# Feed-forward of a hybrid mixer block in two passes over all tokens, with the second mixer sweep between the first pass's column tiles

## The chip, the cores and the metric

The kernel runs on one core of a Trainium2 chip. The metric is the device time of one launch in microseconds (us), the median over the runs of the kernel. Below, TensorE (PE in the profile) does matrix products, VectorE (DVE) and GpSimd (POOL) elementwise work, ScalarE (ACT) activations and copies, and SyncE (SP) issues most DMA transfers.

## What is computed

One layer over x of 2048 tokens by 1024 features: three token mixers on slices of one input projection (a convolution module, a state-space scan "SSD" in both directions, pooling), one output projection, then a gated feed-forward with a 3x3 depthwise convolution on the grid of 32 rows by 64 tokens. Each half ends in a layer norm. Shortened:

```
def _conv_ffn(h, lp, rows, width):
    b, L, _ = h.shape
    val, gate = jnp.split(h @ lp['w_up'], 2, axis=-1)
    gate = _dwconv2d(gate.reshape(b, rows, width, D_FF), lp['ffn_dw_w'], lp['ffn_dw_b']).reshape(b, L, D_FF)
    return (val * jax.nn.gelu(gate)) @ lp['w_down']
...
        mix_x, _, _ = _mixer(_modulate(x, shx1, scx1), lp, st_f, st_b)
        x = _layer_norm(DEEPNORM_ALPHA * x + gx1 * mix_x, ln1_g[l], ln1_b[l])
        f_x = _conv_ffn(_modulate(x, shx2, scx2), lp, rows, GRID_W)
        x = _layer_norm(DEEPNORM_ALPHA * x + gx2 * f_x, ln2_g[l], ln2_b[l])
```

Here `D_FF` is 2816, so `w_up` is 1024 x 5632 and `w_down` is 2816 x 1024. `_mixer` concatenates the three mixers' outputs (256 + 512 + 256 features) and multiplies them by `w_out` (1024 x 1024).

## The kernel before

Tokens are worked on in four chunks of 512 (numbers 0 to 3), in sub-chunks of 128 for the scan. Features lie in tiles of 128 partitions. Every large product is done in three matmuls (`mm3`): each float32 operand is split into a high part (a copy by ScalarE in the matmul's input format) and a low part (the rest, by GpSimd or VectorE), and high by high, high by low and low by high are summed in PSUM. Weights come through `load_w`: SP loads 512 KB into a raw tile (`wr`, two buffers), ScalarE writes `wh`, GpSimd `wl` (three buffers each).

The first sweep goes up through the chunks: input projections, convolutions, the forward scan, pooling. It leaves the forward scan's result (`yf`), the convolution's and pooling's outputs (`yac`) and the scan's inputs (`ub`) in DRAM scratch. The second sweep goes down, chunk 3 to 0. `bwd` runs the backward scan: `first(s)` prepares sub-chunk s, `rest(s)` finishes it, norms, and transposes it (`yt`) into `ybh`/`ybl`. `yac` loads and splits the other mixers' features (`yah`, `yal`). `mix` does the output projection into tiles `o` (two halves of 512 columns by four token tiles), adds the residual (`mix`, `xt`), norms, and transposes (`ht`) into the scratch `h2T`, the feed-forward's input.

Then `ffn_chunk` runs once for each chunk, 3 to 0, all its work in one go. `ffn_h2` reloads `h2T` and splits it (`h2h`, `h2l`, 576 tokens: the chunk and one grid row). For each of 22 column tiles: the gate product `ug` (24 matmuls), its copy into `gbuf`, which holds ten grid rows, nine convolution taps in a PSUM tile `fa` (the first by ScalarE, L863, eight by VectorE, L867), gelu into `fg`, the value product `uv` (24 matmuls) and `g = uv * fg` (L875). Gate rows that the next chunk needs are kept in `gcar`. All 22 tiles of g stay in SBUF. Then the down projection: two halves of 512 columns, in each four PSUM tiles `d` and 22 blocks k, for which ScalarE writes `gh` and VectorE `gl` (L897; three buffers each), 12 matmuls a block. At the end VectorE multiplies by the gate row (`fm`, L911), adds to the residual `r` (L912), and norms (L781, L918, L919). The residual tiles are loaded from scratch and scaled (L882 to L884).

The kernel is written on a framework that gives every tile its semaphores and orders each engine's instructions itself, from a timeline of its own; each engine, SP's list of DMAs among them, then runs its list strictly in that order. So the position of a step on each engine is set at build time, not in the source.

Of the kernel before, what the change touches and what calls it, by code (L numbers as in the profile page):

```python
# [7 lines left out]
F32 = mybir.dt.float32  # L8
# [40 lines left out]
class Kern:  # L49
# [3 lines left out]
    def run(self):  # L53
        tc, t = self.tc, self.t
        with ExitStack() as es:
# [3 lines left out]
            self.mm = es.enter_context(tc.tile_pool(name="mm", bufs=4, space=PSUM))  # L59
            for n, b in (("si", 1), ("so", 2), ("lo", 1)):  # L60
                setattr(self, n, es.enter_context(tc.tile_pool(name=n, bufs=b, space=PSUM)))
            self.consts()
            e1, e2, e3 = ExitStack(), ExitStack(), ExitStack()
            self.sp = e1.enter_context(tc.tile_pool(name="sp", bufs=2))
            self.ssd_consts()
            e4, e5 = ExitStack(), ExitStack()
            self.pc = e5.enter_context(tc.tile_pool(name="pc", bufs=2, side="right"))
            self.mod_first()
            self.p1 = e4.enter_context(tc.tile_pool(name="p1", bufs=2))
            self.sweep1()  # L70
            e5.close()
            self.pa = e2.enter_context(tc.tile_pool(name="pa", bufs=2, side="right", reuse_waits="tile"))
            self.ngr = self.row(self.pa, t["norm_row"], "ngr")
            top = self.bwd(NCH - 1)
            e4.close()
            self.p2 = e2.enter_context(tc.tile_pool(name="p2", bufs=2, side="right", reuse_waits="tile"))
            last = self.sweep2(top)
            e1.close()
            self.p3 = e3.enter_context(tc.tile_pool(name="p3", bufs=2, reuse_waits="tile"))
            self.mix(*last)  # L80
            pre = self.ffn_pre()
            e2.close()
            self.p4 = e3.enter_context(tc.tile_pool(name="p4", bufs=2, side="right", reuse_waits="tile"))
            self.ffn(pre)
            e3.close()

# [104 lines left out]
    def mod_half(self, q):  # L191
        nc, t, p1 = self.nc, self.t, self.p1
        acc = self.lp.tile([P, 512], F32, tag="c31", name=f"macc{q}", bufs=4)
        for k in range(KD):
            w = self.lp.tile([P, 512], F32, tag="c31", name=f"wm2_{q}_{k}", bufs=4)
# [13 lines left out]
    def mod_finish(self):  # L209
# [8 lines left out]
        for r, o in ((0, 0), (1, 24)):  # L218
# [19 lines left out]
    def proj(self, w, hs, n, name):  # L238
        ps = self.bank(self.mm, f"ps_{name}")
        for k in range(KD):  # L240
            a = [v[:, k * P : (k + 1) * P] for v in w]
            self.mm3(ps[:, :n], a, [v[:, :n] for v in hs[k]], k == 0, k == KD - 1)
        return ps
# [14 lines left out]
    def dt_path(self, hs, n, key, name):  # L258
# [5 lines left out]
        raw = sp.tile([40, 512], F32, tag="dtraw", name=f"dtr_{name}", bufs=1)  # L264
# [402 lines left out]
    def sweep2(self, top):  # L667
        p2, t = self.p2, self.t
        self.g1r = self.row(p2, self.s["g1"], "g1r")
        for c in reversed(range(NCH)):  # L670
            cur = (c, self.yac(c, top if c == NCH - 1 else self.bwd(c)))
            if c < NCH - 1:
                self.mix(*prev)
# [370 lines left out]
```

## Time and profile before

| | us |
|---|---|
| median of 2 runs | 2694.12 |
| lowest and highest | 2692.11, 2696.13 |
| span of the profiled execution | 2696.6 |
| second sweep, output projection and transposes | 842 to 1158 |
| feed-forward | 1158 to 2676 |
| last norm and stores | 2676 to 2696.6 |

The profiled execution's span is 2.5 us above the median and inside 0.1% of it; times below come from it. The rows of the profile have us from its start. A group row gives line, engine, operation, output and inputs, shapes and count, then busy time, the mean duration of one in ns, and the idle time of the engine ahead of it. The letter q after an engine's name marks its queue, which issues DMAs. TensorE overlaps successive matmuls, so a single one lasts longer than the pitch between two.

### The profile page before, as it was taken

How to read it: one execution, taken by the hardware profiler on the slowest of the kernel's cores; microseconds unless marked ns; L12 is line 12 of the kernel's file. 1: busy time of each engine (PE TensorE's matmuls, PEld its weight loads, DVE VectorE, ACT ScalarE, POOL GpSimd, SP SyncE). 2: the span in 40 equal slices, each digit the busy share in tenths (PEclk: the TensorE clock that was granted, in tenths of full speed). 3: DMA queues.
4: the chain of work that ended last, by engine and by line, in shares of the span. 5: the costliest groups of instructions: out<-in, count | busy, mean ns of one | idle time of the engine just before them, and what ended most of it. 6: DMA issues, size and time to landing. Idle time of an engine off the chain costs nothing.

```text
span 2696.6 us, 31426 instructions
## 1 busy us (share of the span) xinstructions
PE 2452.2 (91%) x11274; PEld 1989.8 (74%) x11274; DVE 1940.6 (72%) x2621; ACT 1132.2 (42%) x1737; POOL 1394.7 (52%) x928
## 2 busy tenths in 40 slices
PE   6886987979877989899999999999999999989996
PEld 3674765757656777688998878878878888878885
DVE  5999997997977965668555496655596664876645
ACT  2544446455645434433334323334333343233342
POOL 3536456565654664645446455455454464555444
PEclk7897998989988999899999999999999999999998
DMA  7653324233345565572234343333343343433332
GB/s 266 198 170 110 101 94 141 88 112 118 99 150 202 164 227 199 158 257 86 87 94 122 94 147 95 94 109 112 94 148 94 94 117 94 156 92 97 101 94 70
DMA packets 125837, 347.00 MB, mean 129 GB/s; under 512 B 19680, under 2 KB 24176, under 8 KB 125680
## 3 DMA queue, kind: packets, MB, share of 16 engines
q1 hardware_dynamic: 121072, 336.60, 39.9%
q10 hardware_dynamic: 4608, 8.39, 1.0%
q8 instruction: 88, 1.44, 0.2%
q14 instruction: 69, 0.57, 0.1%
HBM read 298.63 MB, written 46.31 MB: 128 GB/s over the span
## 4 chain that ended last, share of the span: by engine, by line
PE 55%; DVE 11%; DMA 3%; POOL 2%; issue 1%; ACT 1%; ACTq 0%; SPq 0%; POOLq 0%; DVEq 0%
PE d L108 6%; PE d L110 6%; PE d L109 6%; PE ug L108 5%; PE ug L109 5%; PE ug L110 5%; PE uv L108 5%; PE uv L110 5%; PE uv L109 5%; PE o L108 1%; PE o L109 1%; PE o L110 1%; DVE rq_l L119 1%; DVE fa L867 1%; DVE xt L764 1%
## 5 line engine op out<-in xcount | busy, mean ns | idle before, releaser
L867 DVE SCALAR_TENSOR_TENSOR fa<-gbuf,cols,fa 128x512 f32<-128x512 f32 x704 | 524.2, 753 | 236.1 <-ACT fa L863 200.2
L897 DVE TENSOR_TENSOR gl<-g,gh 128x512 fp32r<-128x512 f32 x176 | 197.2, 1129 | 230.8 <-ACT gh L896 213.5
L96 POOL TENSOR_TENSOR wl_d<-wr_d,wh_d 128x1024 fp32r<-128x1024 f32 x88 | 217.6, 2473 | 229.9 <-ACT wh_d L95 229.8
L96 POOL TENSOR_TENSOR wl_uv<-wr_uv,wh_uv 128x1024 fp32r<-128x1024 f32 x88 | 222.4, 2527 | 202.4 <-ACT wh_uv L95 202.4
L96 POOL TENSOR_TENSOR wl_ug<-wr_ug,wh_ug 128x1024 fp32r<-128x1024 f32 x88 | 217.2, 2468 | 207.4 <-ACT wh_ug L95 207.4
L108 PE MATMUL ug<-h2h,wh_ug 128*128 128x512 f32 (+3 forms) x880 | 311.0, 353 | 14.6 <-DVE g L875 12.5
L109 PE MATMUL ug<-h2l,wh_ug 128*128 128x512 f32 (+3 forms) x880 | 310.0, 352 | 0.0
L110 PE MATMUL ug<-h2h,wl_ug 128*128 128x512 f32 (+3 forms) x880 | 309.7, 352 | 0.0
L108 PE MATMUL uv<-h2h,wh_uv 128*128 128x512 f32 x704 | 278.8, 396 | 8.4 <-DVE g L875 7.8
L108 PE MATMUL d<-wh_d,gh 128*128 128x512 f32 x704 | 278.7, 396 | 1.2 <-ACT fg L869 1.2
L109 PE MATMUL uv<-h2l,wh_uv 128*128 128x512 f32 x704 | 278.7, 396 | 0.0
L110 PE MATMUL uv<-h2h,wl_uv 128*128 128x512 f32 x704 | 278.7, 396 | 0.0
L109 PE MATMUL d<-wl_d,gh 128*128 128x512 f32 x704 | 277.7, 394 | 0.0
L110 PE MATMUL d<-wh_d,gl 128*128 128x512 f32 x704 | 267.7, 395 | 0.0
L573 DVE SCALAR_TENSOR_TENSOR c<-gl,cols,c 128x512 f32<-128x512 f32 (+1 forms) x240 | 252.7, 1071 | 2.1 <-ACT c L571 1.1
L896 ACT ACTIVATE gh<-g 128x512 fp32r<-128x512 f32 x176 | 110.9, 630 | 268.1 <-PE d L109 242.6
L108 PEld LDWEIGHTS ug<-h2h,wh_ug 128*128 128x128 f32 x880 | 167.5, 190 | 37.4 <-DVE g L875 14.2
L95 ACT ACTIVATE wh_ug<-wr_ug 128x1024 fp32r<-128x1024 f32 x88 | 93.2, 1059 | 227.5 <-PE uv L109 206.4
L109 PEld LDWEIGHTS ug<-h2l,wh_ug 128*128 128x128 f32 x880 | 167.5, 190 | 20.4
L110 PEld LDWEIGHTS ug<-h2h,wl_ug 128*128 128x128 f32 x880 | 167.4, 190 | 19.0
L95 ACT ACTIVATE wh_uv<-wr_uv 128x1024 fp32r<-128x1024 f32 x88 | 93.3, 1060 | 164.1 <-PE ug L109 116.8
L108 PEld LDWEIGHTS uv<-h2h,wh_uv 128*128 128x128 f32 x704 | 132.9, 189 | 39.0 <-DVE g L875 8.2
(376 smaller groups left out, 5629.9 us busy)
## 6 DMA issues: line engine op xcount, KB each, us to landing
wr_ug<-in_w_up SPq DMA_DIRECT2D x88, 512.0 KB, 3.6
wr_uv<-in_w_up SPq DMA_DIRECT2D x88, 512.0 KB, 3.6
wr_d<-in_w_dn SPq DMA_DIRECT2D x88, 512.0 KB, 3.6
wm<-in_w_mod SPq DMA_DIRECT2D x64, 256.0 KB, 3.0
wr_x<-in_w_x SPq DMA_DIRECT2D x32, 512.0 KB, 3.7
wr_o<-in_w_o SPq DMA_DIRECT2D x32, 512.0 KB, 4.5
wm<-in_w_mod SPq DMA_DIRECT2D x16, 512.0 KB, 8.4
x_c<-in_xT SPq DMA_DIRECT2D x32, 256.0 KB, 3.7
```

Source lines behind the costliest of these rows:

```text
L95: nc.scalar.activation(hi, src, AF.Copy)
L96: nc.gpsimd.tensor_tensor(lo, src, hi.bitcast(F32), AL.subtract)
L108: nc.tensor.matmul(out, a[0], b[0], start=first, stop=False)
L109: nc.tensor.matmul(out, a[0], b[1], start=False, stop=False)
L110: nc.tensor.matmul(out, a[1], b[0], start=False, stop=last)
L119: nc.vector.tensor_tensor(q, r, r, AL.mult)
L573: nc.vector.scalar_tensor_tensor(acc[:, :n], gl[:, j, k : k + n], w[k], acc[:, :n], AL.mult, AL.add)
L764: nc.vector.scalar_tensor_tensor(xs[i][:, hsl], xs[i][:, hsl], ALPHA, m, AL.mult, AL.add)
L867: nc.vector.scalar_tensor_tensor(acc, G[:, dr : dr + 8, dc : dc + GW], wc[i], acc, AL.mult, AL.add)
L896: nc.scalar.activation(gh, gt[k], AF.Copy)
L897: nc.vector.tensor_tensor(gl, gt[k], gh.bitcast(F32), AL.subtract)
```

## The change

The feed-forward is cut in two passes over all tokens. Pass 1, `ffn_up`, goes through chunks 3, 2, 1, 0: gate, convolution and value product of each column tile, and g is stored to DRAM (`gs`). So that no row of the next chunk is needed, a chunk's convolution and value product are shifted by 128 tokens: chunk 3 does 384 tokens of its own, chunks 2 and 1 do 512, of which 128 belong to the chunk above, and chunk 0 does 640 as two spans of 320. Three gate rows pass from chunk to chunk through DRAM (`gc`, tile `car`). The input tiles `h2h`, `h2l` hold 640 tokens and have 12 buffers. Pass 2, `ffn_down`, again goes through 3 to 0: it reads g from DRAM once for each half of the columns, and has all eight PSUM banks for `d`. The row broadcasts (`g2r`, `agr`, `abr`, `l2g`, `l2b`) are loaded between the passes.

The backward scan and output projection of chunk 3 run alone ahead of pass 1. Those of chunks 2, 1, 0 become a generator, `back`, of which one step is taken after each column tile of the chunk before. In it the output projection is by features: eight tiles `ps_o_f` of 128 features by 512 tokens, with the residual taken from x transposed (`rt`), the gate a column (`g1a`), and four transposes each (`rT`) back to token rows. `yac` has one buffer. Scan inputs are loaded per sub-chunk.

```
+            hs = self.ffn_h2(NCH - 1)
+            for c in reversed(range(NCH)):
+                side = self.back(c - 1) if c else iter(())
+                for _ in self.ffn_up(c, hs):
+                    next(side, None)
+                for _ in side:
+                    pass
+                if c:
+                    hs = self.ffn_h2(c - 1)
...
+                self.banks(e6, (("dn", 8),))
+                self.p4 = e6.enter_context(tc.tile_pool(name="p4", bufs=2, reuse_waits="tile"))
+                self.ffn_rows()
+                for c in reversed(range(NCH)):
+                    self.ffn_down(c)
...
     def yac(self, c, cat):
...
-            yr = p2.tile([P, 512], F32, tag="yac", name=f"yac{c}_{j}")
+            yr = self.mx.tile([P, 512], F32, tag="yac", name=f"yac{c}_{j}", bufs=1)
...
+        rt = []
+        for f in range(8):
+            x = self.mx.tile([P, 512], F32, tag="rt", name=f"rt{c}_{f}", bufs=3)
+            nc.sync.dma_start(x, t["xT"][f, :, cs])
+            ps = self.proj(self.load_w(t["w_o"][f], f"o{c}_{f}"), cat, CH, f"o{c}_{f}", (0, 1, 6, 7, 2, 3, 4, 5))
+            nc.vector.scalar_tensor_tensor(x, ps, self.g1a[:, f : f + 1], x, AL.mult, AL.add)
+            rt.append(x)
+            if f:
+                turn(f - 1)
+            yield
...
+    def ffn_up(self, c, hs):
+        nc, t, p3 = self.nc, self.t, self.p3
+        n = CH if c == NCH - 1 else CH + P
+        v0 = P if c else 0
+        spans = [(v0, n - v0)] if c else [(0, n // 2), (n // 2, n // 2)]
         for f in range(NF):
...
+            nc.sync.dma_start(self.s[f"gs{c}"][f, :, v0:CH], g[:, 0 : CH - v0])
+            if n > CH:
+                nc.sync.dma_start(self.s[f"gs{c + 1}"][f, :, 0:P], g[:, CH - v0 : n - v0])
+            yield
...
+                    g = p4.tile([P, 512], F32, tag="gr", name=f"gr{c}_{hf}_{k}", bufs=6)
+                    nc.sync.dma_start(g, self.s[f"gs{c}"][k])
                     gh = p4.tile([P, 512], F32R, tag="gh", name=f"gh{c}_{hf}_{k}", bufs=3)
                     gl = p4.tile([P, 512], F32R, tag="gl", name=f"gl{c}_{hf}_{k}", bufs=3)
-                    nc.scalar.activation(gh, gt[k], AF.Copy)
-                    nc.vector.tensor_tensor(gl, gt[k], gh.bitcast(F32), AL.subtract)
+                    nc.scalar.activation(gh, g, AF.Copy)
+                    nc.vector.tensor_tensor(gl, g, gh.bitcast(F32), AL.subtract)
```

PSUM, eight banks of 512 columns, was shared as mm 4, si 1, so 2, lo 1; in pass 1 it is mm 3, cv 2 (the convolution's), si 1, so 1, lo 1. SP's list grows from 845 to 1315 entries, TensorE's shrinks from 10345 to 10197, and ScalarE's table loads go from 39 to 55.

What the change does to the order shows at three places. In these rows a name with numbers is a tile (`g_8` the g of column tile 8, `wr_ug_10` the raw gate weights of tile 10), and `scr_` marks DRAM scratch. First SP's list where the row broadcasts are loaded. Before, in the first chunk of the feed-forward:

```order
L775 DMA scr_h2T_63<-h_0_4_9185 128x512
L775 DMA scr_h2T_63<-h_0_5_9193 128x512
L664 DMA g2r<-scr_g_59 128x1024
L664 DMA agr<-in_ln_rows 128x1024
L664 DMA abr<-in_ln_rows 128x1024
L664 DMA l2g<-in_ln_rows 128x1024
L664 DMA l2b<-in_ln_rows 128x1024
L775 DMA scr_h2T_63<-h_0_6_9201 128x512
L775 DMA scr_h2T_63<-h_0_7_9209 128x512
L882 DMA r_3_0_11602<-scr_x1n_82 128x1024
```

And in the new kernel, at the end of pass 1:

```order
L882 DMA scr_gs_65<-g_21_17565 128x512
L884 DMA scr_gs_73<-g_21_17565 128x128
L685 DMA g2r<-scr_g_59 128x1024
L685 DMA agr<-in_ln_rows 128x1024
L685 DMA abr<-in_ln_rows 128x1024
L685 DMA l2g<-in_ln_rows 128x1024
L685 DMA l2b<-in_ln_rows 128x1024
L892 DMA r_3_0_17646<-scr_x1n_88 128x1024
L892 DMA r_3_1_17650<-scr_x1n_88 128x1024
L892 DMA r_3_2_17654<-scr_x1n_88 128x1024
L892 DMA r_3_3_17658<-scr_x1n_88 128x1024
L905 DMA gr_0_0_17672<-scr_gs_89 128x512
```

The five broadcasts and four loads of r, which stood among the transposed tiles' stores and the up weights, now stand behind the store of the last g of pass 1 and ahead of the first g that pass 2 reads.

Second, VectorE's list at the end of a chunk's down projection. Before, chunk 3's norm, with the next chunk's first convolution tile behind it (`fa`):

```order
L918 SCALAR_TENSOR_TENSOR r_3_0_11602<-r_3_0_11602,mv_l_3_0_12489,l2g 128x1024
L783 BN_AGGR mv_l_3_2_12525<-st_l_3_2_12522 128x2
L115 TENSOR_SCALAR rv_l_3_1_12510<-mv_l_3_1_12507 128x1
L918 SCALAR_TENSOR_TENSOR r_3_1_11606<-r_3_1_11606,mv_l_3_1_12507,l2g 128x1024
L783 BN_AGGR mv_l_3_3_12543<-st_l_3_3_12540 128x2
L119 TENSOR_TENSOR rq_l_3_0_12496<-rr_l_3_0_12494 128x1
L918 SCALAR_TENSOR_TENSOR r_3_2_11610<-r_3_2_11610,mv_l_3_2_12525,l2g 128x1024
L867 SCALAR_TENSOR_TENSOR fa_0_12648<-gbuf_9270,cols,fa_0_12648 128x512
L918 SCALAR_TENSOR_TENSOR r_3_3_11614<-r_3_3_11614,mv_l_3_3_12543,l2g 128x1024
```

In the new kernel, the same end of chunk 3 in pass 2:

```order
L803 BN_STATS st_l_3_0_18618<-r_3_0_17646 128x6
L909 TENSOR_TENSOR gl_0_2_18761<-gr_0_2_18758,gh_0_2_18760 128x512
L923 TENSOR_TENSOR fm_1_3_18615<-d_1_3_18143,g2r 128x512
L803 BN_STATS st_l_3_1_18636<-r_3_1_17650 128x6
L924 TENSOR_TENSOR r_3_2_17654<-r_3_2_17654,fm_1_2_18612 128x512
L805 BN_AGGR mv_l_3_0_18621<-st_l_3_0_18618 128x2
L909 TENSOR_TENSOR gl_0_3_18779<-gr_0_3_18776,gh_0_3_18778 128x512
L924 TENSOR_TENSOR r_3_3_17658<-r_3_3_17658,fm_1_3_18615 128x512
L805 BN_AGGR mv_l_3_1_18639<-st_l_3_1_18636 128x2
L803 BN_STATS st_l_3_2_18654<-r_3_2_17654 128x6
L134 TENSOR_SCALAR rv_l_3_0_18624<-mv_l_3_0_18621 128x1
L930 SCALAR_TENSOR_TENSOR r_3_0_17646<-r_3_0_17646,mv_l_3_0_18621,l2g 128x1024
```

Between the norm's instructions now stand the `gl` of the next chunk's down projection, in place of the taps `fa`.

Third, SP's list where a side chunk's `yac` tiles are loaded, in the new kernel (the other mixers' features of chunk 1, during pass 1 of chunk 2):

```order
L882 DMA scr_gs_81<-g_8_10647 128x384
L884 DMA scr_gs_89<-g_8_10647 128x128
L854 DMA car_14_11358<-scr_gc_90 128x192
L700 DMA yac_0_10680<-scr_yac_70 128x497
L702 DMA yac_0_10680<-scr_yac_78 128x15
L775 DMA rt_0_10709<-in_xT 128x512
L775 DMA rt_1_10826<-in_xT 128x512
L775 DMA rt_2_10949<-in_xT 128x512
L728 DMA zsr_3_12623<-scr_zs_61 128x512
L700 DMA yac_1_10687<-scr_yac_70 128x497
L702 DMA yac_1_10687<-scr_yac_78 128x15
L700 DMA yac_6_10694<-scr_yac_70 128x497
```

And TensorE's list at the start of that projection:

```order
L129 MATMUL uv_8_128_10648<-h2h_7_9588,wl_uv_8_10643 128x512
L369 MATMUL bps_b_3_12398<-ident,ubr_3_12385 128x128 x2
L372 MATMUL bps_b_3_12398<-ubr_3_12385 128x128 x2
L428 MATMUL yd_b_0_10561<-xdt_b_0_10326,E_b_0_10298 128x64 x8
L127 MATMUL ps_o_0_10717<-yah_0_10683,wh_o_0_10712 128x512
L127 MATMUL ug_9_10751<-h2h_0_9539,wh_ug_9_10746 128x512
```

In before the loads of `yac_0` (here of chunk 0) stood among loads of x and output weights:

```order
L749 DMA xt_2_7606<-in_x 128x1024
L749 DMA xt_3_7608<-in_x 128x1024
L683 DMA yac_0_8356<-scr_yac_62 128x497
L685 DMA yac_0_8356<-scr_yac_68 128x15
L683 DMA yac_1_8363<-scr_yac_62 128x497
L685 DMA yac_1_8363<-scr_yac_68 128x15
L102 DMA wr_o_0_3_8426<-in_w_o 128x1024
```

What moved: the `yac` loads now stand behind the store of the g of tile 8, and TensorE comes to the first matmul of `ps_o_0` between the value product of tile 8 and the gate product of tile 9.

307 lines of the change are left out of this document (140 added, 167 removed).

## The prediction, made before the changed kernel was run

> **What bounds the kernel now.** I read the totals first, then the stretches after the first sweep, then the chain of waits through them, and last the groups of instructions by line. The page's totals:
>
> ```profile
> span 2696.6 us, 31426 instructions
> PE 2452.2 (91%) x11274; PEld 1989.8 (74%) x11274; DVE 1940.6 (72%) x2621; ACT 1132.2 (42%) x1737; POOL 1394.7 (52%) x928
> ```
>
> TensorE is the bound: a change pays where it removes TensorE's idle time, and costs where it makes some. The stretches (the first number after the span is its length, then PE, PEld, DVE, ACT and POOL busy, the granted clock, the DMA share, GB/s):
>
> ```profile
> 842.00:1158.00 316.00, 279.51 (x1356) 227.71 (x1356) 222.15 (x391) 131.86 (x255) 178.97 (x125) 0.93 0.60 199
> 1158.00:1240.00 82.00, 76.26 (x458) 69.09 (x459) 64.05 (x93) 30.42 (x44) 39.06 (x27) 0.98 0.56 184
> 1482.80:1550.20 67.40, 67.40 (x291) 54.21 (x290) 30.80 (x36) 26.56 (x36) 29.35 (x12) 1.00 0.33 95
> 1550.20:1617.60 67.40, 62.91 (x262) 50.41 (x261) 63.34 (x85) 19.39 (x24) 35.15 (x20) 0.95 0.45 148
> 1752.40:1819.80 67.40, 66.24 (x284) 53.00 (x284) 39.65 (x54) 25.87 (x34) 34.71 (x26) 1.00 0.38 108
> 1954.60:2022.00 67.40, 62.94 (x260) 50.57 (x259) 63.53 (x80) 22.76 (x30) 35.59 (x25) 0.95 0.47 148
> 2359.00:2426.40 67.40, 59.79 (x264) 50.95 (x265) 53.29 (x73) 25.42 (x34) 34.84 (x28) 0.95 0.32 91
> ```
>
> The third row is dense: 291 matmuls in 67.40 us, a pitch of 0.2316 us for 512 columns. The first is the second sweep. Its output projection alone, the same view of tile `o`, and its first 38 us:
>
> ```profile
> 842.00:1158.00 316.00, 204.49 (x768) 147.12 (x768) 18.80 (x29) 0.93 0.60 199
> ...
> 842.00:880.00 38.00, 31.70 (x151) 26.19 (x152) 27.30 (x44) 18.56 (x46) 19.49 (x16) 0.87 0.61 214
> ```
>
> Dense, the 768 would take 768 x 0.2316 = 177.9 us; everything else there was busy for 279.5 - 204.5 = 75.0. So the sweep loses at least 316 - 177.9 - 75.0 = 63 us. The start of the feed-forward lost 82.0 - 76.3 = 5.7. The chunk boundaries, by matmuls missing against the dense row, lost 29, 7 and 31 pitches, so 6.7, 1.6 and 7.2 us; the last one idled 67.4 - 59.8 = 7.6. Together 92 us.
>
> **What the change removes.** The side work of chunks 2, 1, 0 (backward scan, output projection, transposes) now stands between matmuls of the first pass, and a chunk's last column tile no longer precedes its down projection. I book all 92 us as removed: 2696.6 - 92 = 2604.6. The waits that return are put back one by one.
>
> **What it adds to TensorE's work.** The output projection by features needs 128 more transposes (8 tiles x 4 x 4 chunks). Pieces of the chain of waits:
>
> ```profile
> 1186.15 0.87 PE ht L772 x8
> ...
> 1202.74 1.28 ACT L869
> 1204.04 0.61 ACT fg L869
> 1204.66 0.70 DVE g L875
> ```
>
> Eight transposes took 0.87 us, so 128 take 14: 2618.6. Shifting by 128 tokens narrows chunk 3's value matmuls to 384 columns and makes chunk 0's 2 x 320. The gate rows by form (mean ns last before the idle column):
>
> ```profile
> L108 PE MATMUL ug<-h2h,wh_ug 128*128 128x512 f32 x352 | 141.4, 402 | 8.9 <-DVE g L875 8.9
> L108 PE MATMUL ug<-h2h,wh_ug 128*128 128x256 f32 x176 | 50.4, 286 | 3.6 <-DVE g L875 3.6
> ```
>
> That is 0.45 ns a column: 22 x 24 x 128 columns less is 31 us, and 31 more in chunk 0. Net 0.
>
> **The waits that it makes, in five places.** Durations are from these groups (count, busy us, mean ns), from two moments of VectorE's timeline, and from issue-to-landing times (the last number, us):
>
> ```profile
> L867 DVE SCALAR_TENSOR_TENSOR fa<-gbuf,cols,fa 128x512 f32<-128x512 f32 x704 | 524.2, 753 | 236.1 <-ACT fa L863 200.2 <-PE ug L110 13.6
> L96 POOL TENSOR_TENSOR wl_ug<-wr_ug,wh_ug 128x1024 fp32r<-128x1024 f32 x88 | 217.2, 2468 | 207.4 <-ACT wh_ug L95 207.4
> L897 DVE TENSOR_TENSOR gl<-g,gh 128x512 fp32r<-128x512 f32 x176 | 197.2, 1129 | 230.8 <-ACT gh L896 213.5 <-PE d L109 15.1 <-PE d L110 1.5
> L119 DVE TENSOR_TENSOR rq_l<-rr_l 128x1 f32<-128x1 f32 x32 | 30.2, 945 | 2.7 <-POOL rr_l L117 2.7
> L884 DVE TENSOR_TENSOR r<-r,abr 128x1024 f32<-128x1024 f32 x16 | 28.7, 1811 | 0.0
> L919 DVE SCALAR_TENSOR_TENSOR r<-r,rs_l,l2b 128x1024 f32<-128x1024 f32 x12 | 27.2, 2290 | 0.0
> L912 DVE TENSOR_TENSOR r<-r,fm 128x512 f32<-128x512 f32 x28 | 22.7, 810 | 0.0
> L911 DVE TENSOR_TENSOR fm<-d,g2r 128x512 f32<-128x512 f32 x32 | 21.5, 682 | 16.9 <-PE d L110 16.9
> L883 DVE TENSOR_TENSOR r<-r,agr 128x1024 f32<-128x1024 f32 x16 | 21.5, 1361 | 0.0
> L781 DVE BATCH_NORM_STATS2 st_l<-r 128x6 f32<-128x512 f32 x32 | 21.1, 670 | 0.0
> L918 DVE SCALAR_TENSOR_TENSOR r<-r,mv_l,l2g 128x1024 f32<-128x1024 f32 x12 | 20.9, 1742 | 0.0
> ```
>
> ```profile
> 1545.58 0.69 DVE L897 TENSOR_TENSOR gl<-g,gh 128x512 fp32r<-128x512 f32 x1 [1.65 <-ACT gh L896]
> ...
> 1563.01 1.27 DVE L918 SCALAR_TENSOR_TENSOR r<-r,mv_l,l2g 128x1024 f32<-128x1024 f32 x1
> ...
> 1569.76 3.28 DVE L918 SCALAR_TENSOR_TENSOR r<-r,mv_l,l2g 128x1024 f32<-128x1024 f32 x1
> ```
>
> ```profile
> wr_ug<-in_w_up SPq DMA_DIRECT2D x88, 512.0 KB, 3.6
> ...
> scr_h2T<-h SPq DMA_DIRECT2D x32, 256.0 KB, 4.0
> h2r<-scr_h2T SPq DMA_DIRECT2D x32, 256.0 KB, 3.1
> ...
> yac<-scr_yac SPq DMA_DIRECT2D x12, 248.5 KB, 3.8
> ```
>
> ```profile
> L95 ACT ACTIVATE yah<-yac x16: 613/630/636, 841.2 to 1057.8; 128x512 fp32r<-128x512 f32 x16
> L96 POOL TENSOR_TENSOR yal<-yac,yah x16: 1257/1292/1796, 841.9 to 1058.5; 128x512 fp32r<-128x512 f32 x16
> ```
>
> *1. Chunk 3 alone.* Its scan and projection still have no cover. The first 38 us of the sweep idled 6.3 and ran at 0.87 of the clock (4.9): 11 us come back. Then LayerNorm stands open:
>
> ```profile
> 928.20 0.69 DVE mix L763
> ...
> 946.89 0.33 PE ht L772
> ```
>
> From the end of a projection to the first transpose took 18.7 us; the residual arithmetic in it (about 6) now mostly runs tile by tile, so 13. Store, load and split of the first tile (4.0 + 3.1 + 1.3) make 8, and 3 us of half clock after the pause: 24. Taken 35; low 25 (the pause covered like other transposes), high 48 (18.7 in full, the store at 9).
>
> *2. Starts of chunks 2, 1, 0.* SP now puts each h2T store and its reload in one order. After the last transpose the way back takes about 10 us (0.7 + 4.0 + 0.7 + 3.1 + 1.3), and some 36 matmuls (8 us) stand there to cover it, but with the earlier tiles also late. Low 5 in all (the start in the trace lost 5.7); high 30 (10 each); taken 12, nearer the measured start.
>
> *3. `yac` before the side projections.* In SP's order the load of yac_0 stands behind the store of g_8, and its tile has one buffer. g_8 comes 8.5 us after ug_8 (copy and first tap as two more ScalarE passes of 0.6, eight taps 6.0, gelu 0.6, product 0.7), or 9.8 with a table load of 1.28 ahead of gelu, where scan functions ran between; TensorE has 7.7 us until the first projection matmul (24 matmuls of uv_8, 5.6, and scan work for about 2), so g_8 is 0.8 to 2.1 late, taken 1.5; three issues 1.0, landing 3.8, split 0.6: 6.9 us idle. The next three loads follow each other at 3.8 + 0.4 + 0.6 + 1.3 = 6.1, so 18.4, against 58 matmuls x 0.2316 = 13.4: 5 more. Taken 12 for each of three chunks, 36. Low 0 (queues ahead of TensorE); high 60 (8 us more, by loads that land late).
>
> *4. From pass 1 to pass 2.* SP issues the store of g_21, then five row broadcasts and four r loads, and only then gr_0_0: nine times 512 KB, 4.72 MB. In before the same nine stood under dense work:
>
> ```profile
> 1190.00:1215.00 25.00, 22.79 (x135) 20.21 (x135) 20.70 (x27) 12.06 (x19) 11.05 (x9) 1.00 0.85 297
> ```
>
> At 297 GB/s they take 15.9 us; g_21 comes 4.5 us after the last matmul (1.2 + 16 taps of 0.56, see below, + 0.6 + 0.7, so 11.5 after ug_21, less 48 value matmuls of 320 columns at 0.145, 7.0), two issues 0.8, gh and gl 1.8, half clock 1: taken 24. Low 15 (rows land beside each other and gr early); high 33 (VectorE does its four L893 and three L894, 10.9 us, ahead of gl_0_0). The Trainium skill, page "DMA: Bandwidth & Descriptors", section "Specifications", gives about 358 GB/s for one core: an estimate of 13.2 us, 2.7 less in the sum. The row is an average over 25 us and doesn't contradict it.
>
> *5. Pass 2's chunk boundaries.* Before, convolutions of the next chunk gave VectorE 5.6 us of matmuls between them; now every block of 12 matmuls (2.78 us) needs a gl. In the new order, up to gl_0_13, VectorE does 4 x (0.682 + 0.810 + 0.670 + 1.742 + 2.290 + 0.945) + 2 x (1.361 + 1.811) = 34.9 us and 12 gl, 13.5: 48.4 against 13 blocks, 36.1. TensorE waits 12 us at each of three boundaries: 36. Low 0 (below); high 54 (all four r of the next chunk ahead, 6 more each). The Trainium skill, page "GPSIMD Engine Reference", section "1. Specifications", says that GpSimd shares its SBUF interface with VectorE and contends with VectorE instructions of two SBUF inputs. L918 at 1.27 and 3.28 us within 7 us agrees with it; were every L918 as slow as the second, 4 x 1.54 x 3 = 18 us would come on top.
>
> **Costed at nothing.** Some 470 more DMAs on SP: none by themselves, for weights are asked well ahead (R4 below). Some 70 MB of g written once and read twice: pass 2 asks for 256 KB per 2.78 us beside 256 KB of weights, under 200 GB/s, and 297 was seen. Chunk 0's convolution has 16 taps of 320: at 0.56 us each (L883 and L912 give 1.08 ns a column between 512 and 1024, so 320 columns take 0.75 of 512) they make 9.0 in a tile of 12.5, hidden; at 0.753 it would be 13 us with the products, 0.5 x 22 = 11 exposed. Three mm banks for four hold three 5.6 us tiles against a chain of 8.5 to 9.8. Extra ACT table loads (16 x 1.3) lie in an engine 42% busy. Copies of gate rows leave POOL, the L763 products leave VectorE: neither bounds.
>
> **The sum.** 35 + 12 + 36 + 24 + 36 = 143: 2618.6 + 143 = 2761.6 against the profiled 2696.6; the median, 2694.12, is 2.5 lower, so 2759. All low: 25 + 5 + 0 + 15 + 0 = 45, 2661. All high: 48 + 30 + 60 + 33 + 54 = 225, 2841.
>
> **Rivals.**
> - R1, VectorE runs free in pass 2. With gl at 0.69 and L918 at 1.27 (first timeline rows) the 48.4 us become about 30, under 36.1; place 5 vanishes: 2759 - 36 = 2723. For it: both rows are of this trace. Against it: the means are 1.129 and 1.742, and POOL splits weights all through pass 2.
> - R2, the other side: the `yac` chain is hidden. It needs TensorE to be 12 us behind the queues when the projection starts; then place 3 is nothing: 2723, no change. For it: SP issues ahead by a tile or more. Against it: g_8 is late by its own length.
> - R3, faster: all five places together under 24 us, so under 2640. Only if the loads run far ahead everywhere.
> - R4, SP's one queue starves the weights. In SP's order the load of wr_uv_10 stands behind the store of g_8, three tiles (16.7 us) before its use, less g_8's lateness and the issues between, some 4: 12.5. It needs 3.6 + 2.5 and ScalarE's copy of about 1, 7.1. From a further delay of 5.4 us at SP (a store that waits for g) each us more costs 88 tiles 1 us: with one, 2759 + 88 = 2847. Against it: stores wait for g of two tiles back.
>
> **How the numbers follow.** 2% is about what a measurement of this kernel can tell from no change: bounds 2640 and 2748. Forecast 0.46, of it 0.38 above 2748 and 0.08 below (some place smaller); R1 0.16; R2 0.20; R4 0.10; R3 0.08. Slower 0.38 + 0.10 = 0.48; same 0.08 + 0.16 + 0.20 = 0.44; faster 0.08. The range is that of the bounds, 2661 to 2841; it leaves R3 and R4 out, 0.18. For the forecast alone 2735 to 2800.
>
> **What would show it.** Right: TensorE idle for about 12 us at the first projection matmul of each side chunk, released by yah; idle of over 20 us between uv_21 and the first d; gl releasing d for about 12 us at three boundaries; dense tiles elsewhere. Wrong: those idle times absent; or ug matmuls waiting for wh or wl inside pass 1 (R4); or more than 2 us lost per column tile in chunk 0.

## The result and the profile after

The changed kernel takes 2781.55 us, the median of two runs (2777.97 and 2785.14), against 2694.12 before: a ratio of 1.0317, with a 95% interval of 1.0269 to 1.0365. The forecast was 2759 and its range 2661 to 2841, so the side and the size are right; the terms behind them are less so. The page's totals of the changed kernel, whose profiled execution has a span of 2783.4 us:

```profile
span 2783.4 us, 32662 instructions
PE 2487.5 (89%) x11401; PEld 2020.6 (73%) x11401; DVE 1905.6 (68%) x2787; ACT 1178.0 (42%) x1807; POOL 1346.9 (48%) x818
```

The span grew by 86.8 us. TensorE's busy time grew by 2487.5 - 2452.2 = 35.3, of which 14 are the 128 new transposes. The rest fits slowed work behind the new pauses: after the longest of them, which ends at 2249.3, matmuls of 512 columns follow each other at 0.427 us for some 6 us, against 0.2316 in dense stretches (this is the half clock below), and the granted clock over the span fell from 0.952 to 0.942. TensorE's idle time grew by the other 51.5. The other engines are no busier in sum than before. So TensorE is still the bound and lost its time in pauses. The stretches of it (columns as in the prediction):

```profile
842.00:950.00 108.00, 79.38 (x342) 62.00 (x343) 42.19 (x90) 31.52 (x52) 40.65 (x30) 0.82 0.41 136
1060.00:1085.00 25.00, 18.43 (x91) 15.90 (x90) 10.21 (x20) 7.04 (x12) 10.53 (x9) 0.80 0.56 167
1225.00:1305.00 80.00, 71.25 (x347) 59.11 (x346) 43.92 (x66) 47.42 (x81) 46.22 (x30) 0.98 0.59 181
1575.00:1675.00 100.00, 87.91 (x403) 69.58 (x402) 62.47 (x90) 54.15 (x95) 53.18 (x34) 0.97 0.54 168
1925.00:1970.00 45.00, 37.38 (x174) 30.75 (x175) 23.64 (x41) 18.58 (x28) 23.42 (x15) 0.92 0.47 147
1985.00:2200.00 215.00, 215.00 (x1223) 196.29 (x1223) 143.77 (x307) 79.14 (x119) 86.63 (x51) 1.00 0.38 116
```

The last row is chunk 0's column tiles: 215 us without a gap, although its convolutions are two spans of 320. The others are chunk 3 alone, the first side projection, and the starts of chunks 2, 1 and 0. What TensorE waited for from 842 to 2230 and in pass 2, in the view of waits (us in total, times, longest):

```profile
PE ps_o L127 <- ACT yah L114: 26.3, 7, 7.3
PE ug L127 <- ACT h2h L114: 16.3, 9, 6.0
PE ht L792 <- ACT h L794: 6.0, 7, 1.4
PE ht L792 <- DVE rv_l L134: 6.0, 1, 6.0
...
PE d L127 <- ACT gh L908: 22.0, 1, 22.0
PE d L129 <- DVE gl L909: 9.4, 6, 3.2
PE d L129 <- DVE rq_l L140: 3.2, 1, 3.2
```

These are the five places of the prediction, with their releasers: `yah` (place 3, and in chunk 3), `h2h` (place 2), the norm ahead of `ht` (place 1), the first `gh` of pass 2 (place 4) and `gl` inside the norm (place 5). No wait for weights stands among them.

Waits alone leave out the half clock that follows. So I counted the loss at each place: the length of the stretch, less every matmul there at the pitch that its width has in dense stretches (0.2316 us for 512 columns) and every transpose at 0.109. Such a count moves by a few us with the pitch that is taken for the scan's small matmuls.

| place | predicted, us | measured, us |
|---|---|---|
| losses of before after 842, removed | -92 | -106 |
| new transposes | 14 | 14 |
| first sweep, ends later | 0 | 7 |
| 1: chunk 3 alone | 35 | 46, and 8 in its first column tiles |
| 2: starts of chunks 2, 1, 0 | 12 | 41 (12, 16, 13) |
| 3: `yac`, three side chunks | 36 | 25 (8, 10, 7) |
| 4: from pass 1 to pass 2 | 24 | 25 |
| 5: pass 2's boundaries | 36 | 19 |
| sum | 65 | 79 of the 86.8 |

The other 8 us lie in small pieces between these places.

### The profile page after: what moved, and what is told of

The parts are those of the page before. It is cut to its first block, busy times and chain, and to the rows that moved or that the text cites. A ratio compares the mean times of both kernels' runs of the same rounds, so it can differ in the third digit from the quotient of the medians.

```text
span 2783.4 us, 32662 instructions
## 1 busy us (share of the span) xinstructions
PE 2487.5 (89%) x11401; PEld 2020.6 (73%) x11401; DVE 1905.6 (68%) x2787; ACT 1178.0 (42%) x1807; POOL 1346.9 (48%) x818
## 5 line engine op out<-in xcount | busy, mean ns | idle before, releaser
L873 DVE SCALAR_TENSOR_TENSOR fa<-gbuf,cols,fa 128x512 f32<-128x512 f32 (+2 forms) x880 | 537.4, 645 | 315.3 <-ACT fa L869 302.0
L127 PE MATMUL uv<-h2h,wh_uv 128*128 128x512 f32 (+2 forms) x880 | 309.9, 353 | 4.3 <-ACT gbuf L859 3.8
L129 PE MATMUL uv<-h2h,wl_uv 128*128 128x512 f32 (+2 forms) x880 | 309.6, 352 | 0.0
L128 PE MATMUL uv<-h2l,wh_uv 128*128 128x512 f32 (+2 forms) x880 | 309.0, 351 | 0.0
L127 PE MATMUL ug<-h2h,wh_ug 128*128 128x512 f32 x704 | 289.9, 412 | 20.6 <-ACT h2h L114 16.3
L909 DVE TENSOR_TENSOR gl<-gr,gh 128x512 fp32r<-128x512 f32 x176 | 183.5, 1054 | 170.7 <-ACT gh L908 152.3
L128 PE MATMUL ug<-h2l,wh_ug 128*128 128x512 f32 x704 | 284.9, 405 | 2.7 <-POOL h2l L115 2.7
L129 PE MATMUL ug<-h2h,wl_ug 128*128 128x512 f32 x704 | 283.5, 403 | 0.0
L129 PE MATMUL d<-wh_d,gl 128*128 128x512 f32 x704 | 265.1, 400 | 12.6 <-DVE gl L909 9.4
L128 PEld LDWEIGHTS uv<-h2l,wh_uv 128*128 128x128 f32 x880 | 166.6, 189 | 18.2
L129 PEld LDWEIGHTS uv<-h2h,wl_uv 128*128 128x128 f32 x880 | 166.3, 189 | 16.4
```

Of the source, the lines that this page charges most:

```text
L127: nc.tensor.matmul(out, a[0], b[0], start=first, stop=False)
L128: nc.tensor.matmul(out, a[0], b[1], start=False, stop=False)
L129: nc.tensor.matmul(out, a[1], b[0], start=False, stop=last)
L873: nc.vector.scalar_tensor_tensor(acc, G[:, dr : dr + nr, dc : dc + GW], wc[i], acc, AL.mult, AL.add)
L909: nc.vector.tensor_tensor(gl, g, gh.bitcast(F32), AL.subtract)
```

## The experiments

All times are medians, and each ratio is against the kernel before, run beside it on the same chip. The experiments ran on four chips, on which the kernel before took 2691.1 to 2695.1 us, so a difference between two of them can be off by up to some 4 us where they ran on different chips.

**The `yac` loads early (place 3).** The raw tiles get a pool of their own with four buffers and are loaded at the start of the scan:

```
     def bwd(self, c, cat):
+        self.yraw = {}
+        for j in (0, 1, 6, 7):
+            yr = p2.tile([P, 512], F32, tag="yac", name=f"yac{c}_{j}", bufs=4)
...
+            nc.sync.dma_start(yr[:, :n], self.s[f"yac{c}"][src, :, LAG : LAG + n])
...
+            self.yraw[j] = yr
     def yac(self, c, cat):
-            yr = self.mx.tile([P, 512], F32, tag="yac", name=f"yac{c}_{j}", bufs=1)
+            yr = self.yraw[j]
```

> The four yac tiles of a side chunk get a buffer each and are loaded ahead of its scan, not behind the store of g_8. In the changed kernel TensorE idled 6.4, 7.3 and 5.2 us before ps_o<-yah in the three side chunks, and the 25 us around each lost 8.4, 9.9 and 7.1 us with the half clock. If the late yac loads are the cause (place 3), these losses go: 25 us less, about 2757 us. Rival: another input of that matmul (wh_o, ybh) or the scan is late as well, and the wait only changes its name: 2775 to 2782 us.

It took 2753.05 us, ratio 1.023 (1.0215 to 1.0246): 28.5 us less than the changed kernel's 2781.55. Its waits from 950 on:

```profile
PE ug L127 <- ACT h2h L114: 15.7, 9, 5.6
PE uv L127 <- ACT gbuf L863: 3.8, 4, 1.5
PE ps_o L127 <- ACT yah L114: 3.7, 3, 1.5
```

The 26.3 us for `yah` became 3.7, and nothing took their place: the wait for h2h stayed (16.3 and 15.7). But the edit moves chunk 3's loads as well. The two profiled executions differ by 32.5 us, and by the same count about 19 of them come from the three side projections (26 to 7), 10 from chunk 3, and 4 from the starts. So place 3 is shown, at some 19 us of its 25, and part of place 1 went with it.

**Row broadcasts late (place 4).** `ffn_rows` and all r loads move behind the products of the first half:

```
-                self.ffn_rows()
                 for c in reversed(range(NCH)):
                     self.ffn_down(c)
...
+            if hf == 0:
+                if c == NCH - 1:
+                    self.ffn_rows()
+                for i in range(4):
+                    r = p4.tile([P, 1024], F32, tag="r1", name=f"r1_{c}_{i}", bufs=4)
...
```

> The five row broadcasts and the r loads are moved from the start of pass 2 to behind the first half of its first chunk's products. In the changed kernel the first d waited 22.1 us: gr_0_0 was issued 6.9 us after the last store of g and landed 10.1 us after that, behind 4.7 MB. If these bytes are the cause (place 4), the wait falls to the end of g_21 (3.7 us after the last matmul), one issue, a landing of 3.3 and a split of 1.3, so about 9 us: 13 us less, about 2768 us. Rival: gr is late because its scratch was just written, or the rows then hold up gr in the middle of the first half: 2778 to 2785 us.

It took 2780.01 us, 1.0325 (1.0307 to 1.0343): no gain, though the wait itself did what the first theory said, from 22.0 us to 9.7. How that wait came about, SP's timeline of the changed kernel (start, duration, issue):

```profile
2231.15 0.38 SPq L882 DMA_DIRECT2D scr_gs<-g  x1
...
2232.06 0.47 SPq L685 DMA_DIRECT2D g2r<-scr_g  x1
...
2234.87 2.66 SPq L892 DMA_DIRECT2D r<-scr_x1n  x4
2238.50 17.77 SPq L905 DMA_DIRECT2D gr<-scr_gs  x10
```

and ScalarE's:

```profile
2248.64 1.99 ACT L908 ACTIVATE gh<-gr 128x512 fp32r<-128x512 f32 x3 [18.28 <-DMA gr<-scr_gs]
```

The store of the last g went out at 2231.2, the first gr only at 2238.5, and it landed at 2248.6, ten us later; SP spent the 6.4 us ahead of that issue on the nine transfers. The place was right; but with every chunk's r scaled in the middle of its first half, VectorE's order was worse at the later boundaries: my count of losses fell by 10 us up to 2290 and rose by 7 behind it, and the waits for VectorE in pass 2 rose from 12.6 to 17.3 us. Most of the gain was given back later.

To separate the two, only chunk 3's rows and loads are moved, on top of the early `yac` loads:

```
+        if c < NCH - 1:
+            resid()
...
+                if c == NCH - 1 and hf == 0 and kp == 4:
+                    resid()
```

> On top of the early yac loads (2753 us), the row broadcasts and chunk 3's r loads alone are moved into the first half of pass 2's first chunk; the other chunks keep their r loads where they were. In the run with all r loads moved the first wait of pass 2 fell from 22.1 to 9.7 us, but the whole gained 1.5 us, since later boundaries lost 8 us more. If that give-back came from the r work of chunks 2 to 0, it stays away here: 2753 - 11 = 2742 us. Rival: any wait saved at the start of pass 2 comes back as waits for gl in the first chunk: 2750 to 2755 us.

2736.98 us, 1.0162 (1.0147 to 1.0177): 16 less than 2753. The give-back did come from the r work of the other chunks.

**The side work sooner (place 2).** Three steps of the generator for every two column tiles:

```
-                for _ in self.ffn_up(c, hs):
-                    next(side, None)
+                for f, _ in enumerate(self.ffn_up(c, hs)):
+                    for _ in range(2 if f % 2 == 0 else 1):
+                        next(side, None)
```

> Three steps of the side generator are taken for every two column tiles instead of two, so a side chunk's last transposes and h2T stores come some 7 tiles (about 80 us) before the next chunk starts. The chunk starts lost 12, 16 and 13 us in the changed kernel (waits of ug for h2h up to 6.0 us, and the half clock behind them). If the way through h2T is the cause (place 2), about 30 us of these 41 go: about 2750 us. Rival: the side work is now denser on VectorE and TensorE waits for convolutions in the first tiles instead, or the starts wait for the split's buffers, not for h2T: 2775 to 2790 us.

2775.98 us, 1.0315 (1.0299 to 1.033): 5.6 us less, the rival's answer, but not for one cause alone. The starts did lose their waits for h2h: from 20 us ahead of a chunk's first gate matmul to 80 behind it, the three starts lose 6 us by the same count, where the changed kernel loses 44 in these windows. New waits arose among the denser scan steps. ScalarE's timeline some 40 us ahead of chunk 2's start, in the last column tiles of chunk 3:

```profile
1224.01 2.46 ACT L366 ACTIVATE E_b<-E_b,cum_c 128x128 f32<-128x128 f32 x8 [4.02 <-DMA E_b<-scr_arow]
1227.43 1.28 ACT L367 ACT_TABLE_LOAD   x1
1228.73 1.06 ACT L367 ACTIVATE E_b<-E_b 128x1024 f32<-128x1024 f32 x1
1229.69 2.43 ACT L366 ACTIVATE E_b<-E_b,cum_c 128x128 f32<-128x128 f32 x8
1232.14 1.28 ACT L875 ACT_TABLE_LOAD   x1
1233.43 0.49 ACT L875 ACTIVATE fg<-fa 128x384 f32<-128x384 f32 x1
```

In its view of waits, TensorE from 1225 to 1245:

```profile
PE ug L128 <- DVE g L882: 7.6, 1, 7.6
```

ScalarE runs its list in order. It stood 4.0 us for a scan input, worked on two of the scan's `E_b` tiles, with one exponential, and loaded two function tables (1.28 us each) before it came to the gelu `fg`; VectorE's product waited for that, and TensorE 7.6 us for the product's PSUM tile. Scan steps have such chains on ScalarE and VectorE; output projection steps are nearly TensorE's alone. So in a later kernel (early `yac`, late rows of chunk 3, more gl buffers) only the projection's steps are doubled:

```
+                    for _ in range(2 if f in (8, 9, 10, 11) else 1):
```

> On top of the seven gl buffers, two steps of the side generator are taken at column tiles 8 to 11, in the output projection, which is TensorE's work alone; the scan's steps stay one a tile. The last transposes then come 7 tiles ahead of the next chunk's start. If h2T sets the starts (ug waits 16 us for h2h, losses of 12 to 16 us each at three starts), 25 us go: about 2696 us, if the boundaries went too. Rival as in the run with three steps for two tiles: other queues give back half, 2708 us, or all of it, 2720 us.

2707.32 us, 1.0065 (1.0048 to 1.0081): 19 less than the kernel that it was built on, 2726.53 (below). `h2h` is no longer among the longer waits (0.9 us in all), and the three starts lose 6 us in the windows named above, where they lost 43. So place 2 is shown at its counted size; the expected 25 were not reached in the whole, since other waits grew: 4.2 us for `g` some 23 us ahead of chunk 2's start, and 6.6 for `yah` against 3.7. No run made the scan's steps alone denser, and the run with three steps for two tiles still had the late `yac` loads, so that the scan is the part that can't be made denser is read from its waits.

**No interleaving.** All steps of the generator run behind the chunk's column tiles:

```
                 for _ in self.ffn_up(c, hs):
-                    next(side, None)
+                    pass
```

> The side work of chunks 2, 1 and 0 is written behind each chunk's column tiles instead of one step after each tile; all else as in the changed kernel. If the interleaving does what the prediction booked (it hides the second sweep's waits), this gives back about three quarters of the 63 us of that sweep and adds the open way from the last output matmul to the next chunk's first (about 24 us for chunk 3) three times: 2781 + 47 + 60, near 2885 us, and not under 2830. Rival: the interleaving hides little, since the waits only moved to the starts and to yac: 2770 to 2800 us.

2879.69 us, 1.07 (1.0682 to 1.0719), and 98 above the changed kernel. Its longest waits:

```profile
PE ps_o L127 <- ACT yah L114: 31.5, 13, 5.1
PE ht L792 <- DVE rv_l L134: 23.8, 4, 6.0
PE ht L792 <- ACT h L794: 10.8, 12, 1.0
PE yo_b L422 <- DVE state_b L416: 9.4, 10, 1.6
```

The 6.0 us ahead of `ht`, which the changed kernel has once, for chunk 3, stand here four times. The interleaving is worth 98 us; the two passes without it would be 7% slower than before. It is not what costs.

The other extreme, each side chunk written ahead of the column tiles that it runs beside, with early `yac`:

> On top of the early yac loads (2753 us), each side chunk is written ahead of the column tiles that it runs beside, so its steps come as early as they can and h2T is done two thirds of a chunk before it is read. If the chunk starts are set by h2T (they lost about 36 us in the run with early yac), 25 us go; the run with two steps a tile gave back 14 us of such a gain in dense stretches of scan work on ScalarE and VectorE, so about 2742 us. Rival: dense scan steps stall TensorE as in the second sweep before the change (three quarters of 63 us): 2780 to 2800 us.

2818.56 us, 1.0468 (1.0453 to 1.0484): 66 more than 2753. That is on the rival's side and above its 2800. The build put the scan and the projection of each side chunk ahead of the column tiles, with none beside them: for chunk 1, from 1279 to 1378, TensorE has no matmul of `ug` or `uv` at all. Only the last transposes still run beside column tiles. So nothing covers the scan's waits, as in the second sweep of before; the longest of them, from 842 to 2300:

```profile
PE yt L743 <- DVE yfr L740: 11.4, 5, 5.9
PE xps_b L383 <- DVE gtm_b L377: 9.8, 7, 2.7
PE yd_b L428 <- DVE y_b L424: 8.8, 5, 3.3
```

The run thus repeats what the one without interleaving showed; it doesn't tell what dense scan steps do beside column tiles.

**Chunk 3 alone (place 1).** Chunk 2's scan is put beside chunk 3's projection, and every later side step half a chunk earlier:

```
-            for _ in self.mix(NCH - 1, cat):
-                pass
+                below = self.bwd(NCH - 2, nxt)
+                for _ in self.mix(NCH - 1, cat):
+                    next(below, None)
...
+    def back(self, c, cat, nxt):
+        yield from self.mix(c, cat)
+        if c:
...
+                yield from self.bwd(c - 1, nxt)
```

> On top of the early yac loads (2753 us), the side work is shifted by half a chunk: chunk 2's backward scan runs beside chunk 3's output projection, and pass 1 of a chunk runs beside the next chunk's projection and then the scan below it (h2h and h2l with 9 buffers for 12). Chunk 3 alone (place 1) lost about 46 us in the changed kernel and its norm and reload chain now have chunk 2's scan and projection beside them; the later starts (place 2) find h2T long done. If these two places cost what the trace says, some 25 and 25 us go: near 2705 us. Rival: the scan of chunk 2 (20 us of TensorE and its waits) now lies in the stretch without column tiles and costs what it saves: 2735 to 2755 us.

2766.83 us, 1.0277 (1.0257 to 1.0298): 14 slower than with early `yac` alone, and above the rival's range too. The norm ahead of `ht` still held TensorE for 5.95 us and the scan's waits now lay in the open: from 850 to 1050 my count of losses is 61 us, against 38 with early `yac` alone. So what the early loads had left of place 1 didn't shrink. No run here took away the 6.0 us ahead of `ht` or the rest of it, so that share is read from the trace and not shown by removal.

**Pass 2's boundaries (place 5).** First the norm's scaling moves from VectorE to ScalarE and GpSimd:

```
-                nc.vector.scalar_tensor_tensor(r, r, mv[:, 0:1], self.l2g, AL.subtract, AL.mult)
-                nc.vector.scalar_tensor_tensor(r, r, rsd, self.l2b, AL.mult, AL.add)
...
+                nc.scalar.activation(r, r, AF.Identity, bias=nb, scale=rsd)
+                nc.gpsimd.tensor_tensor(r, r, self.l2g, AL.mult)
+                nc.gpsimd.tensor_tensor(r, r, self.l2b, AL.add)
```

> On top of the early yac loads (2753 us), the last norm of chunks 3, 2 and 1 takes its scaling from VectorE: ScalarE does (x - mean) / std, GpSimd the gain and bias. This takes 4 x (1.6 + 1.3) = 11.6 us a boundary from VectorE and puts eight passes of some 2.5 us on GpSimd. If VectorE's order of gl among the norm is what TensorE waits for there (place 5, 19 us in three boundaries), about 12 us go: 2741 us. Rival: GpSimd's passes stand ahead of wl and TensorE waits for weights: 2753 to 2780 us.

2798.43 us, 1.0393 (1.0374 to 1.0411): 45 slower. Neither theory named the way. TensorE waited 38.5 us for `gl` and next to nothing for `wl`. VectorE's and GpSimd's timelines in the first boundary:

```profile
2362.21 7.55 POOL L937 TENSOR_TENSOR r<-r,l2g 128x1024 f32<-128x1024 f32 x3
2369.72 2.34 POOL L938 TENSOR_TENSOR r<-r,l2b 128x1024 f32<-128x1024 f32 x1
2372.02 2.34 POOL L115 TENSOR_TENSOR wl_d<-wr_d,wh_d 128x1024 fp32r<-128x1024 f32 x1
...
2361.52 0.16 DVE L139 TENSOR_TENSOR rq_l<-rq_l,rv_l 128x1 f32<-128x1 f32 x1
...
2365.11 2.36 DVE L138 TENSOR_TENSOR rq_l<-rr_l 128x1 f32<-128x1 f32 x1
2367.50 2.28 DVE L139 TENSOR_TENSOR rq_l<-rq_l,rv_l 128x1 f32<-128x1 f32 x1
2369.81 0.15 DVE L140 TENSOR_SCALAR rq_l<-rq_l 128x1 f32<-128x1 f32 x1
2370.00 2.07 DVE L141 TENSOR_TENSOR rs_l<-rr_l,rq_l 128x1 f32<-128x1 f32 x1
2372.11 2.26 DVE L935 SCALAR_TENSOR_TENSOR nb<-mv_l,rs_l 128x1 f32<-128x1 f32 x1
...
2376.20 10.87 DVE L913 TENSOR_TENSOR gl<-gr,gh 128x512 fp32r<-128x512 f32 x4 [1.23 <-ACT gh L912]
```

The same step of one column with two tensors to read (L139) takes VectorE 0.16 us at 2361.5, ahead of GpSimd's passes, and 2.28 us beside them, about as long as one whole GpSimd pass; the step with one tensor (L140) takes 0.15 us even there. L139, L141 and L935 each end within 0.02 us of the end of a GpSimd instruction, so they seem to have waited for it, and four `gl` behind them took 10.9 us together, where one alone takes 0.69. The Trainium skill, page "SBUF — State Buffer", section "SBUF: two separate sides", says that VectorE and GpSimd share a pair of ports as an exclusive lock, held for a whole instruction, which a VectorE instruction with two SBUF inputs needs. The trace agrees beside GpSimd's long passes, with these numbers.

Then the other way: more buffers, so that VectorE has `gl` done ahead (`gh` goes from 3 to 7 and `gr` from 6 to 8 as well):

```
-                    gl = p4.tile([P, 512], F32R, tag="gl", name=f"gl{c}_{hf}_{k}", bufs=3)
+                    gl = p4.tile([P, 512], F32R, tag="gl", name=f"gl{c}_{hf}_{k}", bufs=7)
```

> On top of early yac loads and late rows for chunk 3 (2737 us), pass 2 gets seven buffers each for gh and gl and eight for gr (three and six before), so VectorE can be six blocks (16.7 us) ahead when a chunk's norm begins, not two. If the boundaries' 6.3 us (a wait of 3.2 for gl some 31 us behind the boundary, and half clock) come from VectorE falling behind TensorE there, they go: 16 us less, near 2721 us. Rival: the order of gl among the norm sets the wait whatever the buffers: 2735 to 2738 us.

2726.53 us, 1.0131 (1.0116 to 1.0146): 10.5 less than 2737. The waits of 3.2 us at the boundaries went, though about 2 us remain at each by my count, now with waits for `wl_d` of up to 1.9 us (5.8 in four). Place 5 was VectorE falling behind, as the prediction had it: TensorE had waited for `gl` there, and no longer does. The three buffer counts were changed together, so which of them was needed is not shown.

**The last waits.** On top of the doubled projection steps, the `yac` splits get their own buffers and run inside the scan (h2h and h2l with 11 buffers):

```
+            if n == 2 and c < NCH - 1:
+                self.yac(c, cat)
             rest(s)
```

> On top of the o-step run (2707 us), the splits of the side chunks' yac tiles get buffers of their own and are written into the third scan step, not behind the scan (h2h and h2l with 11 buffers for 12). That run still waited 3.1 and 2.7 us for yah at two side projections and lost 9.5 us around them. If these waits are only the late split, 8 us go: 2699 us. Rival: ScalarE's splits inside the scan push the scan's own steps back and the wait changes its name: 2705 to 2712 us.

2699.73 us, 1.0026 (1.0015 to 1.0037): the wait for `yah` is gone and 7.6 us with it (the two ran on different chips; against the kernel before beside each, the ratio fell from 1.0065 to 1.0026, some 10 us). And two blocks of g are loaded and split beside the last chunk's column tiles:

```
+            if c == 0 and f == NF - 8:
+                for k in range(NPRE):
...
+                    nc.sync.dma_start(gr, self.s[f"gs{NCH - 1}"][k])
...
+                    self.pre.append((gh, gl))
```

> As the run with early splits, and two blocks of g for pass 2 are loaded and split already beside pass 1's last chunk, in buffers of their own (h2h and h2l with 9 buffers). The first d then needs no load behind the last store of g: two blocks (5.6 us) stand in the 9.9 us wait before d, the third block still comes by that way. If this is the last wait there, 5 to 8 us go: 2693 us, even with the kernel before. Rival: the fewer buffers of h2h hold up the chunk starts by as much: 2699 to 2708 us.

2709.89 us, 1.006 (1.0042 to 1.0077), 10 slower. The 9.9 us pause before the first d became one of 3.2, in which TensorE waited for the last product `g`. Another of 3.2 came 35 us later, for `wl_d`, GpSimd's part of the down weights. The kernel as a whole lost. By my count its chunk starts (1150 to 1300, 1550 to 1650, 1850 to 1950) lost some 28 us against 16, which fits the fewer buffers of h2h (waits for it are back at 4.1 us, and for `h2l` at 4.2); no run changed the buffers alone.

The best of these, 2699.73 us, is 0.26% slower than the kernel before. No version here beats it.

## Why the prediction was right, and where it was not

- *TensorE stays the bound and the time is its pauses.* Right: the span's 86.8 us are 51.5 of idle time and 35.3 of busy time, of which 14 are the transposes.
- *The losses removed: 92 booked, 106 measured.* The second sweep's 63 hold when its small matmuls are counted at the pitch that they have in dense stretches (0.11 us for 64 and 128 columns, 0.215 for the scan's 256). The start of the feed-forward lost 9 by the count, not 5.7, and the four boundaries 26, not 23: the idle time and the missing matmuls that were booked there leave out part of the slowed work. The rest lies in small pieces of the feed-forward.
- *Place 3, 36 against 25.* The mechanism is shown by the early loads, which took some 19 of the 25. The first part was right: 6.4, 7.3 and 5.2 us at the first matmul against 6.9 predicted. The 5 us for the three loads behind it didn't come; the loads landed in 2.7 us, not 3.8, as the page of the changed kernel has it, and were covered:

```profile
yac<-scr_yac SPq DMA_DIRECT2D x12, 248.5 KB, 2.7
```

- *Place 4, 24 against 25.* Right in size and in cause: the nine transfers stood ahead of gr, and moving them took 12.3 us off the wait.
- *Place 5, 36 against 19.* The place was right: the wait comes at 2403.9, 2533.1 and 2662.1, some 31 us behind each boundary, and 13 blocks of `gl` (36 us) were named. TensorE waited 3.2 us each time, not 12. The mis-sized term is the duration: L931 was booked at 2.290 us a piece and took 1.282. In before, six of the twelve took 3.1 to 3.4 us, with GpSimd at work throughout, and six 1.3; in the new order all twelve took 1.28. What in the new order keeps them clear of GpSimd was not tested:

```profile
L931 DVE SCALAR_TENSOR_TENSOR r<-r,rs_l,l2b 128x1024 f32<-128x1024 f32 x12 | 14.9, 1282 | 0.0
L909 DVE TENSOR_TENSOR gl<-gr,gh 128x512 fp32r<-128x512 f32 x176 | 183.5, 1054 | 170.7 <-ACT gh L908 152.3 <-PE d L128 10.5 <-PE d L129 4.2
```

  With the means of the changed kernel's trace (0.676, 0.912, 0.674, 1.629, 1.282 and 0.654, then 1.214 and 1.757, and 1.054 for `gl`) the prediction's own sum gives 41.9 against 36.1, so 6 us a boundary, which is what came. R1's mechanism is half in it, but its sum was wrong: with `gl` at 0.69 and L918 at 1.27 alone, the 48.4 become 41.3 and not 30, so place 5 would have shrunk to 5 us a boundary and not vanished. The mean of `gl` shows that some still ran beside GpSimd, since a `gl` alone takes 0.69 (its median in pass 2).
- *Place 2, 12 against 41.* This is the step that failed. I took a value near the one start in the trace of before (5.7 us), with 36 matmuls as cover. Here ug and uv of the first tile take the new h2h one k at a time, and each k waits for its own way through DRAM and its split. These waits come to 16.3 us. In the rows of the three starts TensorE is idle for 28 us in all, so 12 more went in smaller waits (of `ug` and `uv` for `h2l`, `gbuf` and `g`, of `ht`, and of the next side chunk's scan), and the rest is slowed work. Two runs that bring the side work forward in time show the cause: the waits for h2h went, and the loss at the starts with them. The upper bound of 30 was too low as well.
- *Place 1, 35 against 46 and 8.* Low. The projection of chunk 3 also waited for `yah` (7 us), which the term didn't hold; the early loads took about 10 us off the place.
- *Costed at nothing.* Right for SP's queue (R4: no wait for weights among the longer ones), the 82.6 MB more of DMA traffic, chunk 0's convolutions (215 us without a gap) and three mm banks. Not right for the order of the first sweep, which the new pools changed: it ended 7 us later by my count, and no run tested why.
- *What would show it.* Of the three idle times that the prediction named, the one before the first d came as said (22.0 us for over 20). The one before the side projections came at 5.2 to 7.3 us for about 12, the one for `gl` at 3.2 for about 12. None of the signs of being wrong came.

The terms erred on both sides: places 3 and 5 were 28 us too high and the gain 14 too low; places 1, 2, 4 and the first sweep were 19 + 29 + 1 + 7 = 56 too low. The sum was near because they cancelled in part, and its nearness is no proof of the parts.

## What to carry to other kernels

Interleaving a chained stage into a dense one, one step a tile, was worth 98 us here. Packing the steps closer paid for those that are nearly TensorE's alone: doubling the projection's steps gained 19 us, while three steps for every two tiles, the scan's among them, gained 5.6 with new waits behind the in-order ScalarE and VectorE. Before cutting a loop in two passes, count each buffer that stood full across the old boundary: every one that is now stored, reloaded or split again needs to be asked for a tile ahead, and with a few buffers and loads in a better order most of the loss went (2781.55 to 2699.73 us), though no version was faster than one pass. A saved wait is only a gain when the work that caused it isn't put ahead of the next one, as the late r loads showed.

## What the runs showed of the hardware

VectorE instructions of one column with two tensor inputs took 2.1 to 2.4 us beside GpSimd's passes of 2.3 to 2.5 us and 0.16 ahead of them; one with a single input took 0.15 us. So beside long GpSimd instructions the count of such tiny steps, not their size, was what a stretch cost. And the refill between the passes moved data at 406 GB/s for one core, in this row of the changed kernel (no TensorE work, DMA share above 1):

```profile
2237.00:2247.00 10.00, 0.00 (x0) 0.00 (x0) 2.74 (x3) 0.00 (x0) 2.09 (x2) 0.50 1.02 406
```

The estimate that the prediction made from the Trainium skill's 358 GB/s, page "DMA: Bandwidth & Descriptors", section "Specifications", was 13.2 us for these bytes; the row is faster than that rate, and the measurement decides. Five of the nine transfers spread one row over all partitions, so the row is no clean measure of reading from DRAM.
